# A decoder block in split float32: one contraction tile and four channel tiles multiplied whole

## The chip, the cores and the metric

The kernel runs on one core of a Trainium2 chip. The metric is the device time of one execution in microseconds; the kernel before has a median of 1739.6 us over 3 runs (1739.5 to 1740.47). The engines of the core are named PE (matrix multiply; PEld is its weight load), DVE (vector), ACT (activation and copy), POOL and SP (which here issues nearly all DMAs). Each works through its own instructions in order and waits for the others by semaphores.

## The reference, cut to what matters

One decoder layer on x of 256 tokens by 4096 channels, all in float32:

```
mod = silu(c) @ w_ada + b_ada             -> shift, scale, gate   (4096 -> 3 x 4096)
h   = rmsnorm(x) * (1 + scale) + shift
P   = h @ w_in                            (256 x 4096) @ (4096 x 14336)
y_A = a_b * conv3(a_c * a_x) * silu(a_z)              mixer A, 2048 channels
y_B = silu(layernorm(conv31(b_v * sigmoid(b_g)))) * silu(b_z)   mixer B, 2048 channels
out = rmsnorm(x + gate * ([y_A, y_B] @ w_out))        (256 x 4096) @ (4096 x 4096)
```

## The kernel before

**Split products.** The matrix products keep float32 accuracy by a split. Each weight tile (2 contraction tiles of 128 rows by 512 columns, a "step") is loaded as float32 into a buffer w_r of the pool "raws", which has four buffers. ACT casts it to float32r (w_h, L217) and DVE subtracts (w_l = w_r - w_h, L218). The activations h and y are split the same way (L250 on ACT, L253 on DVE). `products` then issues three matmuls for each contraction tile and each of the two token tiles: high by high, high by low, low by high (L244 to L246). w_h and w_l have three buffers each in the pool "split".

**Order of the work.** w_in is walked in seven blocks of contraction tiles (2, 4, 4, 4, 6, 6, 6 of the 32). In each block all 28 column tiles of 512 are visited; one visit is a "segment". A segment is seeded with the sum so far (L599) and taken off PSUM by ACT or DVE (L615, L610). The last block holds contraction tiles 26 to 31, so each of its 28 segments has three steps, and the third multiplies tiles 30 and 31. Its column tiles come in the order 20, 16, 21, 17, 22, 18, 23, 19, then four rounds of 4, 8, 12, 0 counted up, then 24 to 27. After it w_out is walked in two halves: first contraction tiles 0 to 15 (the channels of mixer A) for all eight output tiles ("pa", eight steps each, taken by L668), then tiles 16 to 31 (mixer B, "pb").

**What runs beside it.** During the last block and pa, the short convolution of mixer A (L438 to L444) makes y in tiles yfA, the convolution of 31 taps of mixer B runs tap by tap as a product on ACT (L500) and an addition on DVE (L503) or as one step on DVE (L496), and DVE sums the columns of the gate's weights (L271, 1 MB each). Two reductions on PE, mu_ps and var_ps (L525), belong to the layer norm, and gate_ps (L300) turns the finished gate.

**What sets the order.** The order on every engine is written by the program itself. `now` counts contraction tiles multiplied. `put` files work under a due count, and `run_due` issues it; the gate sums are fillers, issued when due or when the planner's account of DVE's time (`vec`, with LOW_PART for each subtracted contraction tile) and of the loads has room. `next_w` issues the load, cast and subtraction of a step two steps before its matmuls (AHEAD = 2). A tile of a pool takes the free buffer that was released longest ago, and its first writer waits for that buffer's last reader. The tiles h, x, y, the sums and the convolution's products share the pool "big" of 34 buffers.

Of the kernel before, what the change touches and what calls it, by code (L numbers as in the profile page):

```python
# [22 lines left out]
KT = D // P  # L23
# [49 lines left out]
def _segments():  # L73
# [35 lines left out]
def decoder_block(ctx: ExitStack, tc: tile.TileContext, x, c, w_mod, w_gate, w_in, w_out, xt, pk, final_g, out):  # L109
    nc = tc.nc  # L110
# [58 lines left out]
    plan = [(w_in[e], k, n) for _, e, k0, k1 in SEGS for k, n in _steps(k0, k1)]  # L169
    end_in = sum(n for _, _, n in plan)  # L170
    start_last = sum(k1 - k0 for b, _, k0, k1 in SEGS if b < len(BLOCKS) - 1)
    conv_end = end_in + CONV_END
    plan += [(w_out[dt], k0 + k, KD) for k0 in (0, KT // 2) for dt in range(NDT) for k in range(0, KT // 2, KD)]
    loaded = []
    step = 0
    now = 0
# [2 lines left out]
    vec = load = 0.0  # L179
# [9 lines left out]
    def run_due():  # L189
# [7 lines left out]
        while filler:  # L197
            due, mb, cost, f = filler[0]
            if due > now and (max(vec, t - SLACK) + cost > t + UNIT * KD or max(load, t - SLACK) + mb / RATE > t + UNIT):
                break  # L200
# [6 lines left out]
    def load_w(i):  # L207
        nonlocal vec, load
        src, k, n = plan[i]
        raw = raws.tile([P, KD, CT], F32, tag="r", name=f"w{i}_r")  # L210
        part = slice(k % KD, k % KD + n)
        nc.sync.dma_start(raw[:, part], src[k // KD][:, part])
        if 0 <= i - len(plan) + KT // 2 // KD < HOLD:
            hi, lo = (bigt(f"w{i}_{t}", (P, KD, CT), F32R) for t in "hl")
        else:
            hi, lo = (split.tile([P, KD, CT], F32R, tag=t, name=f"w{i}_{t}") for t in "hl")
        nc.scalar.copy(hi[:, part], raw[:, part])  # L217
        nc.vector.tensor_tensor(out=lo[:, part], in0=raw[:, part], in1=hi[:, part].bitcast(F32), op=ALU.subtract)  # L218
        t = FIRST + UNIT * now
        vec = max(vec, t - SLACK) + LOW_PART * n  # L220
        load = max(load, t - SLACK) + W_LOAD * n / RATE
        return hi, lo

    def next_w():

# [8 lines left out]

    def products(ps, act, parts, k0, n, first, last, tokens=range(NS), seeded=False):

        hi, lo = parts
        for k in range(k0, k0 + n):
            f, l = first and k == k0, last and k == k0 + n - 1
            for s in tokens:  # L240
                out = ps[s] if isinstance(ps, list) else ps[:, s]
                ah, al = (act[k][:, h, s * P:(s + 1) * P] for h in range(2))
                i = k % KD
                nc.tensor.matmul(out, ah, hi[:, i], start=f, stop=False, skip_group_check=seeded)  # L244
                nc.tensor.matmul(out, ah, lo[:, i], start=False, stop=False, skip_group_check=seeded)  # L245
                nc.tensor.matmul(out, al, hi[:, i], start=False, stop=l, skip_group_check=seeded)  # L246

    def hi_part(dst, src):

        nc.scalar.copy(dst[:, :, 0], src)  # L250

    def lo_part(dst, src):
        nc.vector.tensor_tensor(out=dst[:, :, 1], in0=src, in1=dst[:, :, 0].bitcast(F32), op=ALU.subtract)  # L253
# [55 lines left out]
    act_h = {}  # L309

    def h_steps(ks):

        st = {}
        n = len(ks)

        def fetch():
            st["x"] = bigt(f"xc{ks[0]}", (P, n, S))
            nc.sync.dma_start(st["x"], xt[:, ks[0]:ks[0] + n])

        def by_token():  # L320
            nc.vector.tensor_tensor(out=st["x"], in0=st["x"], in1=rstd.unsqueeze(1).broadcast_to([P, n, S]), op=ALU.mult)

        def by_channel():
            for i, k in enumerate(ks):
                nc.scalar.activation(out=st["x"][:, i], in_=st["x"][:, i], func=AF.Identity, scale=gscT[:, k:k + 1], bias=modT[:, k:k + 1])

        def high():
            st["h"] = bigt(f"hT{ks[0]}", (P, n, 2, S), F32R)
            hi_part(st["h"], st["x"])

        def low():
            lo_part(st["h"], st["x"])
            for i, k in enumerate(ks):
                act_h[k] = st["h"][:, i]

        return [(fetch, 0.0), (by_token, 0.3 * n + 0.05), (by_channel, 0.0), (high, 0.0), (low, 0.3 * n + 0.05)]

# [5 lines left out]
    for q in range(4):  # L343
        for s in range(NS):
            t = bigt(f"xn{q}_{s}", (P, 1024))
# [23 lines left out]
    v, y, t = (tiny[:, i] for i in range(3))  # L369
# [25 lines left out]
    vec = load = FIRST - SLACK  # L395
# [19 lines left out]
    yT = {}  # L415
# [7 lines left out]
    def silu_gate_A(i):  # L423

        p, q = acc[4 + i], acc[i]
        tiles, pss = {}, {}

        def turn(j):
            cc = slice(j * P, (j + 1) * P)
            ps = pss[j] = misc(f"psA{4 * i + j}", (P, 2, S))  # L430
            for s in range(NS):
                nc.tensor.transpose(ps[:, 0, s * P:(s + 1) * P], p[:, s, cc], ident)
                nc.tensor.transpose(ps[:, 1, s * P:(s + 1) * P], q[:, s, cc], ident)

        def tap(j):
            if j % 2 == 0:
                tiles[j // 2] = bigt(f"yfA{i}_{j}", (P, 2, S))
            nc.scalar.activation(out=tiles[j // 2][:, j % 2], in_=pss[j][:, 0], func=AF.Copy, scale=caw[:, 4 * i + j, 2:3])  # L438

        def rest(j):  # L440
            y, ct = tiles[j // 2][:, j % 2], 4 * i + j
            for sh in (1, 2):
                nc.vector.scalar_tensor_tensor(out=y[:, sh:], in0=pss[j][:, 0, :S - sh], scalar=caw[:, ct, 2 - sh:3 - sh], in1=y[:, sh:], op0=ALU.mult, op1=ALU.add)
            nc.vector.tensor_tensor(out=y, in0=y, in1=pss[j][:, 1], op=ALU.mult)  # L444
            if j % 2 == 1:
                hi, lo = split_y(2 * i + j // 2, tiles[j // 2])
                put(now + 2, hi)
                put(now + 4, lo, 0.65)

        t = now + 4  # L450
        for j in range(4):
            put(t + A_STEP * j, lambda j=j: turn(j))
            put(t + A_STEP * j + 0.1, lambda j=j: tap(j))
            put(t + A_STEP * j + 2, lambda j=j: rest(j), 1.15)
# [177 lines left out]
    for n, (b, e, k0, k1) in enumerate(SEGS):  # L632
        steps = _steps(k0, k1)
        for j, (k, m) in enumerate(steps):
            parts = begin_step()
# [11 lines left out]
    for i in range(4):  # L647
        for h in range(2):
            t = end_in + NORM_AT + NORM_STEP * (19.5 + 2 * i + h)
# [20 lines left out]
    for dt in range(NDT):  # L670
        ps = pst(f"pa{dt}")
        for k in range(0, KT // 2, KD):
            parts = begin_step()
# [91 lines left out]
    for s in range(NS):  # L765
# [4 lines left out]
        v, y, t = (const.tile([P, 1], F32, name=f"o_{n}{s}") for n in "vyt")  # L770
# [47 lines left out]
```

## Time and profile before

| | |
|---|---|
| median of 3 runs | 1739.6 us |
| the profiled execution | 1735.66 us, span 1733.9 us |
| PE busy | 1635.9 us (94%) |
| DVE busy | 1398.1 us (81%) |
| ACT busy | 1171.9 us (68%) |
| DMA | 526.02 MB, mean 303 GB/s |
| mean granted PE clock | 0.991 |

The page's slices of the span:

```profile
PE   6999999999999999999999999989988988899997
DVE  6888877778777877778777778899999999875666
ACT  5787667666677666666656666999977775564444
DMA  9998999999999999999999999665666778667775
```

Each column is a fortieth of the span (43.3 us), each digit the busy share in tenths. The shares of the whole span are means over parts with different limits, so a change in one part is read from that part alone. A matmul's duration includes a drain that overlaps the next one, so for its cost one looks at the time from start to next start.

### The profile page before, as it was taken

What the parts mean: (1) busy time and instruction counts of PE and PEld (TensorE: products, weight loads), DVE (VectorE), ACT (ScalarE), POOL (GpSimd) and SP (SyncE); (2) the same over time, 40 slices, a digit from 0 to 9 for tenths busy, and PEclk for the clock granted to TensorE, in tenths of its full rate; (3) what the DMA queues carried; (4) which work ended last, traced back from release to release, by engine and by line L of the source; (5) the groups of instructions that cost most, each with busy time, mean ns of one, the idle gap of its engine ahead of it and who ended that gap; (6) DMA issues with size and microseconds to landing.
All of it is one profiled execution on the core that took longest, in us unless ns stands there. A gap on an engine that the chain in (4) does not pass through costs nothing.

```text
span 1733.9 us, 20044 instructions
## 1 busy us (share of the span) xinstructions
PE 1635.9 (94%) x7069; PEld 1321.2 (76%) x7069; DVE 1398.1 (81%) x1409; ACT 1171.9 (68%) x1525; POOL 1.0 (0%) x8
## 2 busy tenths in 40 slices
PE   6999999999999999999999999989988988899997
PEld 3668878888788788887888887777766766778885
DVE  6888877778777877778777778899999999875666
ACT  5787667666677666666656666999977775564444
POOL 0000000000000000000000000000000000000000
PEclk9999999999999999999999999999999999999999
DMA  9998999999999999999999999665666778667775
GB/s 363 373 380 334 370 336 336 331 346 357 342 349 348 358 336 344 348 353 361 338 349 342 349 359 336 205 188 165 194 232 222 286 258 292 240 195 248 242 240 190
DMA packets 122284, 526.02 MB, mean 303 GB/s; under 512 B 13476, under 2 KB 13764, under 8 KB 97608
## 3 DMA queue, kind: packets, MB, share of 16 engines
q1 hardware_dynamic: 121992, 524.36, 83.7%
q8 instruction: 56, 0.92, 0.2%
q10 hardware_dynamic: 192, 0.39, 0.1%
q14 instruction: 44, 0.36, 0.1%
HBM read 520.48 MB, written 4.21 MB: 303 GB/s over the span
## 4 chain that ended last, share of the span: by engine, by line
PE 62%; DVE 19%; issue 8%; ACT 5%; DMA 5%; SPq 0%; DVEq 0%; ACTq 0%
PE ps L246 17%; PE ps L244 17%; PE ps L245 17%; DVE w_l L218 7%; DVE cv L503 4%; DMA w_r<-in_w_in 4%; PE pb L245 3%; PE pb L244 3%; PE pb L246 3%; ACT w_h L217 2%; DVE gate L271 2%; DVE cv L496 2%; DMA mod<-in_w_mod 1%; DVE mod L271 1%; ACT acc L615 1%
## 5 line engine op out<-in xcount | busy, mean ns | idle before, releaser
L218 DVE TENSOR_TENSOR w_l<-w_r,w_h 128x1024 fp32r<-128x1024 f32 (+1 forms) x591 | 704.9, 1196 | 302.6 <-ACT w_h L217 301.9
L217 ACT CAST w_h<-w_r 128x1024 fp32r<-128x1024 f32 (+1 forms) x591 | 609.4, 1032 | 499.8 <-PE ps L246 325.6
L245 PE MATMUL ps<-w_l,hT 128*128 128x512 f32 x1792 | 703.9, 393 | 24.0 <-DVE w_l L218 23.8
L244 PE MATMUL ps<-w_h,hT 128*128 128x512 f32 x1792 | 705.6, 394 | 15.2 <-ACT hT L250 7.9
L246 PE MATMUL ps<-w_h,hT 128*128 128x512 f32 x1792 | 702.5, 392 | 9.5 <-DVE hT L253 9.4
L245 PEld LDWEIGHTS ps<-w_l,hT 128*128 128x128 f32 x1792 | 338.6, 189 | 102.6 <-DVE w_l L218 33.4
L244 PEld LDWEIGHTS ps<-w_h,hT 128*128 128x128 f32 x1792 | 338.4, 189 | 92.5 <-ACT hT L250 8.6
L246 PEld LDWEIGHTS ps<-w_h,hT 128*128 128x128 f32 x1792 | 338.4, 189 | 83.8 <-DVE hT L253 13.5
L615 ACT ACTIVATE acc<-ps 128x1024 f32<-128x1024 f32 x178 | 181.4, 1019 | 0.0
L599 ACT COPY ps<-acc 128x1024 f32<-128x1024 f32 x162 | 164.1, 1013 | 0.0
L500 ACT ACTIVATE pr<-uT,pks 128x254 f32<-128x254 f32 (+23 forms) x384 | 159.3, 496 | 0.0
L271 DVE CUSTOM_DVE_ANT_0 mod<-mod,cB,pks 128x2048 f32<-128x2048 f32 x64 | 150.2, 2346 | 2.7 <-DMA mod<-in_w_mod 2.7
L271 DVE CUSTOM_DVE_ANT_0 mod<-mod,cB,pts 128x2048 f32<-128x2048 f32 x64 | 150.2, 2347 | 2.6 <-DMA mod<-in_w_mod 2.6
L245 PE MATMUL pa<-w_l,yT 128*128 128x512 f32 x256 | 103.1, 403 | 14.2 <-DVE w_l L218 14.2
L503 DVE TENSOR_TENSOR cv<-cv,pr 128x1020 f32<-128x1020 f32 (+11 forms) x96 | 111.3, 1159 | 0.9
L244 PE MATMUL pa<-w_h,yT 128*128 128x512 f32 x256 | 102.6, 401 | 0.0
L246 PE MATMUL pa<-w_h,yT 128*128 128x512 f32 x256 | 101.1, 395 | 0.0
L244 PE MATMUL pb<-w_h,yT 128*128 128x512 f32 x256 | 99.8, 390 | 0.0
L246 PE MATMUL pb<-w_h,yT 128*128 128x512 f32 x256 | 99.6, 389 | 0.0
L245 PE MATMUL pb<-w_l,yT 128*128 128x512 f32 x256 | 99.6, 389 | 0.0
L271 DVE CUSTOM_DVE_ANT_0 gate<-gate,cB,pts 128x2048 f32<-128x2048 f32 x32 | 75.1, 2347 | 0.0
L271 DVE CUSTOM_DVE_ANT_0 gate<-gate,cB,pks 128x2048 f32<-128x2048 f32 x32 | 75.1, 2346 | 0.0
(112 smaller groups left out, 689.4 us busy)
## 6 DMA issues: line engine op xcount, KB each, us to landing
w_r<-in_w_in SPq DMA_DIRECT2D x433, 512.0 KB, 5.3
mod<-in_w_mod SPq DMA_DIRECT2D x128, 1024.0 KB, 7.2
gate<-in_w_gate SPq DMA_DIRECT2D x64, 1024.0 KB, 6.5
w_r<-in_w_out SPq DMA_DIRECT2D x128, 512.0 KB, 4.4
w_r<-in_w_in SPq DMA_DIRECT2D x30, 256.0 KB, 5.7
xn<-in_x SPq DMA_DIRECT2D x8, 512.0 KB, 5.8
xr<-in_x SPq DMA_DIRECT2D x8, 512.0 KB, 6.9
out<-o SPq DMA_DIRECT2D x16, 256.0 KB, 2.4
```

What stands on the lines that cost most here:

```text
L217: nc.scalar.copy(hi[:, part], raw[:, part])
L218: nc.vector.tensor_tensor(out=lo[:, part], in0=raw[:, part], in1=hi[:, part].bitcast(F32), op=ALU.subtract)
L244: nc.tensor.matmul(out, ah, hi[:, i], start=f, stop=False, skip_group_check=seeded)
L245: nc.tensor.matmul(out, ah, lo[:, i], start=False, stop=False, skip_group_check=seeded)
L246: nc.tensor.matmul(out, al, hi[:, i], start=False, stop=l, skip_group_check=seeded)
L271: nc.vector.tensor_tensor_reduce(out=raw, in0=raw, in1=cB[:, q * ROW:(q + 1) * ROW], scale=1.0, scalar=pt if q else bias, op0=ALU.mult, op ...
L496: nc.vector.scalar_tensor_tensor(out=o[:, j, sh:], in0=u[:, j, :S - sh], scalar=cbw[:, 4 * i + j, TAPS - 1 - sh:TAPS - sh], in1=o[:, j, sh ...
L500: nc.scalar.activation(out=pr[:, j, sh:], in_=u[:, j, :S - sh], func=AF.Copy, scale=cbw[:, 4 * i + j, TAPS - 1 - sh:TAPS - sh])
L503: nc.vector.tensor_tensor(out=o[:, :, sh:], in0=o[:, :, sh:], in1=pr[:, :, sh:], op=ALU.add)
L599: nc.scalar.copy(ps, acc[e])
L615: nc.scalar.activation(out=acc[e], in_=ps, func=func)
```

## The change

The last contraction tile of w_in (31) and four of w_out (12 to 15, mixer A's last channels) are multiplied whole: one float32 matmul of the unsplit activations by the unsplit weights w_r takes the place of three split ones. Nothing of those weights is cast or subtracted, and h of tile 31 and y of tiles 12 to 15 are not split. In the third step of a segment of the last block half of the weight tile is split and half is not; in pa the last two of eight steps are whole. The float32 tiles of x (two contraction tiles) and of y (yfA) are kept until their last matmul, and w_r until its step is multiplied. The planner counts LOW_PART only for what is subtracted.

```diff
+WHOLE_IN = (KT - 1,)
+WHOLE_OUT = (12, 13, 14, 15)
...
     def load_w(i):
         src, k, n = plan[i]
+        whole = WHOLE_IN if i < steps_in else WHOLE_OUT
+        ns = sum(j not in whole for j in range(k, k + n))
         raw = raws.tile([P, KD, CT], F32, tag="r", name=f"w{i}_r")
...
-        nc.scalar.copy(hi[:, part], raw[:, part])
-        nc.vector.tensor_tensor(out=lo[:, part], in0=raw[:, part], in1=hi[:, part].bitcast(F32), op=ALU.subtract)
+        if ns:
+            part = slice(k % KD, k % KD + ns)
+            nc.scalar.copy(hi[:, part], raw[:, part])
+            nc.vector.tensor_tensor(out=lo[:, part], in0=raw[:, part], in1=hi[:, part].bitcast(F32), op=ALU.subtract)
         t = FIRST + UNIT * now
-        vec = max(vec, t - SLACK) + LOW_PART * n
+        vec = max(vec, t - SLACK) + LOW_PART * ns
...
-        return hi, lo
+        return hi, lo, raw
...
     def products(ps, act, parts, k0, n, first, last, tokens=range(NS), seeded=False):
...
+                i = k % KD
+                if act[k].dtype == F32:
+                    nc.tensor.matmul(out, act[k][:, s * P:(s + 1) * P], raw[:, i], start=f, stop=l, skip_group_check=seeded)
+                    continue
                 ah, al = (act[k][:, h, s * P:(s + 1) * P] for h in range(2))
...
         def low():
-            lo_part(st["h"], st["x"])
+            lo_part(st["h"][:, :ns], st["x"][:, :ns])
             for i, k in enumerate(ks):
-                act_h[k] = st["h"][:, i]
+                act_h[k] = st["h"][:, i] if i < ns else st["x"][:, i]
...
-            if j % 2 == 1:
+            if ct in WHOLE_OUT:
+                yT[ct] = y
+            elif j % 2 == 1:
```

DVE, around the two whole steps of the second pa tile (weight tiles w477 and w478, tap additions cv3 and a gate sum between them), before:

```order
L218 TENSOR_TENSOR w476_l_10567<-w476_r_10564,w476_h_10566 128x1024
L503 TENSOR_TENSOR cv3_8688<-cv3_8688,pr3_1_10547 128x4x255
L271 ISA gate24_0_10576,pts_103<-gate24_0_10576,cB_104,pks_60 128x2048
L271 ISA pts_103 128x1
L218 TENSOR_TENSOR w477_l_10594<-w477_r_10591,w477_h_10593 128x1024
L503 TENSOR_TENSOR cv3_8688<-cv3_8688,pr3_2_10570 128x4x254
L218 TENSOR_TENSOR w478_l_10618<-w478_r_10615,w478_h_10617 128x1024
L503 TENSOR_TENSOR cv3_8688<-cv3_8688,pr3_3_10597 128x4x253
L218 TENSOR_TENSOR w479_l_10642<-w479_r_10639,w479_h_10641 128x1024
```

The same place on DVE now:

```order
L228 TENSOR_TENSOR w476_l_10425<-w476_r_10422,w476_h_10424 128x1024
L519 TENSOR_TENSOR cv3_8655<-cv3_8655,pr3_1_10405 128x4x255
L284 ISA gate24_0_10434,pts_103<-gate24_0_10434,cB_104,pks_60 128x2048
L284 ISA pts_103 128x1
L519 TENSOR_TENSOR cv3_8655<-cv3_8655,pr3_2_10428 128x4x254
L519 TENSOR_TENSOR cv3_8655<-cv3_8655,pr3_3_10451 128x4x253
L228 TENSOR_TENSOR w479_l_10492<-w479_r_10489,w479_h_10491 128x1024
```

The two subtractions are gone; the additions and the gate sum between them stand as they stood.

SP, the loads that follow the two whole steps w469 and w470 of the first pa tile, with what each waits for (the DMAHW names are semaphores of earlier DMAs), before:

```order
L212 DMA w471_r_10437<-in_w_out 128x1024 [waits DMAHW6_49,DVE_49]
L270 DMA gate23_0_10449<-in_w_gate 128x2048 [waits DMAHW4_49]
L212 DMA w472_r_10464<-in_w_out 128x1024 [waits DMAHW7_49,DVE_49]
L212 DMA w473_r_10489<-in_w_out 128x1024 [waits DMAHW1_49,DVE_49]
L212 DMA w474_r_10515<-in_w_out 128x1024 [waits DMAHW2_49,DVE_49]
L270 DMA gate23_1_10526<-in_w_gate 128x2048 [waits DMAHW0_49]
L212 DMA w475_r_10541<-in_w_out 128x1024 [waits DMAHW3_49,DVE_49]
```

The same loads on SP now:

```order
L217 DMA w471_r_10311<-in_w_out 128x1024 [waits DMAHW6_49,DVE_49]
L283 DMA gate23_0_10323<-in_w_gate 128x2048 [waits DMAHW4_49]
L217 DMA w472_r_10330<-in_w_out 128x1024 [waits DMAHW7_49,DVE_49]
L217 DMA w473_r_10347<-in_w_out 128x1024 [waits DMAHW3_49,DVE_49]
L217 DMA w474_r_10373<-in_w_out 128x1024 [waits DMAHW1_49,PE_49]
L283 DMA gate23_1_10384<-in_w_gate 128x2048 [waits DMAHW0_49]
L217 DMA w475_r_10399<-in_w_out 128x1024 [waits DMAHW2_49,PE_49]
```

The order of the loads is the same; w474 and w475 take the buffers that the whole steps held and wait for PE where they waited for DVE.

## Rows read from the trace of the kernel before

**Rows 1.** Windows: length, then busy us of each engine (instructions), granted clock, DMA share, GB/s.

```profile
core 0: us, PE busy (x) PEld busy (x) DVE busy (x) ACT busy (x) POOL busy (x), PEclk, DMA share, GB/s
1052.00:1096.00 44.00, 42.21 (x193) 34.35 (x192) 34.49 (x33) 32.48 (x47) 0.00 (x0) 1.00 0.82 295
1096.00:1250.00 154.00, 140.58 (x627) 111.69 (x626) 145.79 (x176) 147.74 (x268) 0.00 (x0) 1.00 0.59 184
1250.00:1331.60 81.60, 67.12 (x276) 52.73 (x275) 80.85 (x100) 65.04 (x120) 0.00 (x0) 0.92 0.65 226
1331.60:1461.00 129.40, 116.60 (x485) 92.08 (x485) 129.02 (x141) 96.85 (x175) 0.00 (x0) 0.97 0.77 276
1461.00:1546.20 85.20, 73.61 (x323) 57.80 (x322) 68.14 (x68) 45.17 (x59) 0.00 (x0) 0.98 0.69 231
1546.20:1722.00 175.80, 175.20 (x776) 144.53 (x774) 111.63 (x109) 86.26 (x109) 0.00 (x0) 1.00 0.70 228
```

**Rows 2.** Timeline, ACT: takes of segments and pa tiles: start us, us, instruction.

```profile
1095.97 1.03 ACT L615 ACTIVATE acc<-ps 128x1024 f32<-128x1024 f32 x1
...
1250.12 1.01 ACT L615 ACTIVATE acc<-ps 128x1024 f32<-128x1024 f32 x1
...
1460.92 1.01 ACT L668 COPY o<-pa 128x1024 f32<-128x1024 f32 x1
```

**Rows 3.** Waits from 1096 to 1250: total us, times, longest us.

```profile
PE ps L245 <- DVE w_l L218: 7.2, 8, 1.9
```

**Rows 4.** Waits from 1331.6 to 1461.

```profile
PE pa L245 <- DVE w_l L218: 12.8, 11, 2.1
```

**Rows 5.** Waits from 1461 to 1546.2.

```profile
PE mu_ps L525 <- DVE mu_t L520: 4.3, 1, 4.3
...
PE gate_ps L300 <- DVE gateT L271: 3.0, 1, 3.0
...
PE var_ps L525 <- DVE var_t L520: 2.4, 1, 2.4
```

**Rows 6.** Timeline, PE: first and last of 45 split matmuls in a row.

```profile
1080.02 0.39 PE L244 MATMUL ps<-w_h,hT 128*128 128x512 f32 x1
...
1089.99 0.39 PE L246 MATMUL ps<-w_h,hT 128*128 128x512 f32 x1
```

**Rows 7.** Timeline, PE: float32 matmuls of other shapes (in brackets the wait before).

```profile
3.03 13.99 PE L363 MATMUL cps<-crow,ones 1*128 1x512 f32 x16 [3.03 <-DMA crow<-in_c]
...
1497.82 1.13 PE L525 MATMUL var_ps<-var_t,mean_w 128*128 128x256 f32 x4 [2.35 <-DVE var_t L520]
```

**Rows 8.** Timeline, PE: after a long wait.

```profile
1275.75 0.79 PE L245 MATMUL ps<-w_l,hT 128*128 128x512 f32 x1 [3.50 <-DVE w_l L218]
1276.34 0.63 PE L246 MATMUL ps<-w_h,hT 128*128 128x512 f32 x1
...
1278.05 0.63 PE L244 MATMUL ps<-w_h,hT 128*128 128x512 f32 x1
...
1278.78 0.39 PE L246 MATMUL ps<-w_h,hT 128*128 128x512 f32 x1
```

**Rows 9.** Groups by shape, DVE and ACT: count, busy us, mean ns, idle before.

```profile
L218 DVE TENSOR_TENSOR w_l<-w_r,w_h 128x1024 fp32r<-128x1024 f32 x561 | 685.1, 1224 | 297.3 <-ACT w_h L217 296.7
L218 DVE TENSOR_TENSOR w_l<-w_r,w_h 128x512 fp32r<-128x512 f32 x30 | 20.3, 689 | 5.3 <-ACT w_h L217 5.2
...
L217 ACT CAST w_h<-w_r 128x1024 fp32r<-128x1024 f32 x561 | 591.0, 1055 | 487.5 <-PE ps L246 321.1 <-PE pb L246 65.8 <-PE pa L246 53.5
L217 ACT CAST w_h<-w_r 128x512 fp32r<-128x512 f32 x30 | 18.4, 617 | 12.3 <-DMA w_r<-in_w_in 7.7 <-PE ps L246 4.5
```

**Rows 10.** Timeline, DVE: a subtraction and the instruction after it.

```profile
1376.83 1.22 DVE L218 TENSOR_TENSOR w_l<-w_r,w_h 128x1024 fp32r<-128x1024 f32 x1
1377.96 1.21 DVE L503 TENSOR_TENSOR cv<-cv,pr 128x1012 f32<-128x1012 f32 x1
```

**Rows 11.** DMA issues from 1050 to 1331: count, KB each, median us to landing.

```profile
w_r<-in_w_in SPq DMA_DIRECT2D x78, 512.0 KB, 3.9
gate<-in_w_gate SPq DMA_DIRECT2D x15, 1024.0 KB, 6.1
```

**Rows 12.** DMA issues from 1331 to 1546.

```profile
w_r<-in_w_out SPq DMA_DIRECT2D x65, 512.0 KB, 4.4
```

More of the change, by code (lines that the diff above doesn't have):

```diff
@@ L173, in decoder_block @@
     plan += [(w_out[dt], k0 + k, KD) for k0 in (0, KT // 2) for dt in range(NDT) for k in range(0, KT // 2, KD)]
+    steps_in = sum(len(_steps(k0, k1)) for _, _, k0, k1 in SEGS)
     loaded = []
@@ L212, in load_w @@
         nc.sync.dma_start(raw[:, part], src[k // KD][:, part])
-        if 0 <= i - len(plan) + KT // 2 // KD < HOLD:
+        hi = lo = None
+        if not ns:
+            pass
+        elif 0 <= i - len(plan) + KT // 2 // KD < HOLD:
             hi, lo = (bigt(f"w{i}_{t}", (P, KD, CT), F32R) for t in "hl")
@@ L235, in products @@
     def products(ps, act, parts, k0, n, first, last, tokens=range(NS), seeded=False):
-        hi, lo = parts
+        hi, lo, raw = parts
         for k in range(k0, k0 + n):
@@ L241, in products @@
                 out = ps[s] if isinstance(ps, list) else ps[:, s]
+                i = k % KD
+                if act[k].dtype == F32:
+                    nc.tensor.matmul(out, act[k][:, s * P:(s + 1) * P], raw[:, i], start=f, stop=l, skip_group_check=seeded)
+                    continue
                 ah, al = (act[k][:, h, s * P:(s + 1) * P] for h in range(2))
-                i = k % KD
                 nc.tensor.matmul(out, ah, hi[:, i], start=f, stop=False, skip_group_check=seeded)
@@ L314, in h_steps @@
         n = len(ks)
+        ns = sum(k not in WHOLE_IN for k in ks)
         def fetch():
@@ L328, in high @@
             st["h"] = bigt(f"hT{ks[0]}", (P, n, 2, S), F32R)
-            hi_part(st["h"], st["x"])
+            hi_part(st["h"][:, :ns], st["x"][:, :ns])
         def low():
-            lo_part(st["h"], st["x"])
+            lo_part(st["h"][:, :ns], st["x"][:, :ns])
             for i, k in enumerate(ks):
-                act_h[k] = st["h"][:, i]
+                act_h[k] = st["h"][:, i] if i < ns else st["x"][:, i]
         return [(fetch, 0.0), (by_token, 0.3 * n + 0.05), (by_channel, 0.0), (high, 0.0), (low, 0.3 * n + 0.05)]
```

## The prediction

> **What bounds the kernel now.** I began with the slices of the page: DMA is near full until slice 25 and falls after it, and DVE reads 9 from slice 27 to 34. So the program has three parts with different limits. The change touches only the last block of six (28 segments) and the first half of the output projection (eight tiles "pa"), so I cut exactly that stretch into windows [rows 1]. The cuts lie at the takes that end the fifth segment of the block (1095.97), the twenty-first (1250.12) and the fifth pa tile (1460.92), counted in the code's order [rows 2].
>
> - 1052 to 1096 us, 5 segments: PE busy 42.2 of 44.0, DVE 34.5. PE is the limit.
> - 1096 to 1250, 16 segments: PE 140.6, DVE 145.8, ACT 147.7 of 154.0. All three are nearly full.
> - 1250 to 1331.6, 7 segments: DVE 80.9 of 81.6, PE 67.1, and the clock is 0.92. DVE is the limit.
> - 1331.6 to 1461, 5 pa tiles: DVE 129.0 of 129.4, PE 116.6. DVE is the limit.
> - 1461 to 1546.2, 3 pa tiles: PE 73.6 of 85.2, DVE 68.1. Neither is full: PE waits here three times for a result of DVE that its next instruction in order needs.
> - 1546.2 to 1722, the second half of the projection: PE 175.2 of 175.8. PE is the limit, and the change leaves it alone.
>
> The waits agree. PE waits for the low parts w_l of DVE: 7.2 us in the second stretch, 12.8 in the fourth [rows 3, 4]. In the fifth it waits 4.3 for mu_t, 3.0 for gateT, 2.4 for var_t [rows 5].
>
> **What one matmul costs.** A split product is three matmuls. From 1080.02 to 1089.99 there are 45 starts in a row, 44 steps of 0.2266 us [rows 6], so one token of one contraction tile costs 0.680 us. A float32 matmul of 128x512 with full rows is not in this trace. Two relatives are. The eight matmuls "cps" (one row by 512 columns, float32) appear as 16 records in 13.99 us: two records each, 0.862 us per record once 0.2 for the last one's drain is taken off [rows 7] (0.63 of duration less 0.43 of step [rows 8]). The two "var_ps" matmuls (256 columns) are four records in 1.13 us, 0.242 per record after 0.16 of drain (0.39 less 0.23 [rows 6, 7]). Per 512 columns that is 0.484, so cps at 0.862 must have run at the lower clock, 1.2 GHz; at 2.4 GHz it is 0.431 per record, 0.862 per matmul. The split matmuls at half clock step by 0.4275 (1276.34 to 1278.05 in four steps [rows 8]); four such passes at full clock are 0.855. So the added PE time is 0.175 from that side, 0.18 from cps, 0.288 from var_ps (which started after a wait). I take 0.18, because cps has the longest run of records. There are 28 x 2 = 56 such matmuls in the block and 8 x 4 x 2 = 64 in pa: 120 x 0.18 = 21.6 us on PE, 0.36 per segment and 1.44 per pa tile.
>
> The Trainium skill, "FP8 and Floating Point Precision", section TensorE Precision Notes, says that a true float32 product takes 4 passes through the array. The trace agrees in kind (two records, each of double length), but at the pace of the split matmuls four passes would be 0.906, an estimate from that page, so 0.226 more each and 27 us in all; the sum below would then come out at -8.0 in place of -12.9 (106 of the 120 lie where PE can become the limit, 106 x 0.046 = 4.9).
>
> **What leaves DVE and ACT.** A subtraction of 128x1024 has 1224 ns, of 128x512 689 [rows 9], so each segment frees 0.535 us of DVE. The cast goes from 1055 to 617 ns, 0.438 us of ACT. In pa two of eight steps lose the whole subtraction, which is 1.13 us from start to next start (1376.83 to 1377.96 [rows 10]), so 2.26 per tile on DVE and 2.1 on ACT. Two splits of y go too, 0.69 each on DVE. The low part of h shrinks once; that is nothing here. The planner also issues two gate sums some 30 loads earlier in the block; DVE has them to do all the same, so I count the move at nothing. It gains a little if they land in the 8.2 us in which DVE is idle in the second stretch.
>
> **Stretch by stretch.**
> 1. 5 segments, PE the limit: 5 x 0.36 = **+1.8**.
> 2. 16 segments. PE becomes 140.6 + 5.8 = 146.4, ACT 147.7 - 7.0 = 140.7, DVE 145.8 - 8.6 = 137.2. PE alone allows 154.0 - 146.4 = -7.6; nothing at all is gained if the small waits of three full engines stay as they are. I take **-3**: today 154.0 is 6.3 above the fullest engine, and 151 keeps 4.6 of it.
> 3. 7 segments, DVE the limit with PE far behind (67.1 + 2.5): 7 x 0.535 = **-3.7**. Ends: -3.7 and -2.
> 4. 5 tiles. DVE sheds 5 x 2.26 + 1.4 = 12.7. PE is 116.6, less 3.9 that the half clock cost (0.03 x 129.4), plus 7.2: 119.9, so PE stops the gain at -9.5. I take **-7**, some 2.5 us of waits for w_l staying of 12.8. The lower end is -2.
> 5. 3 tiles: PE +4.3. The three waits hold 9.7 us and all are for DVE, which arrives 6.8 us lighter. Ends: +4.3 if they stay, -2.5 if 6.8 goes. I take **-1**.
> 6. The second half and the tail: 0. Their instructions are the same; I leave 1 us either way, since the last two whole steps of pa still hold buffers when it begins.
>
> Sum: 1.8 - 3 - 3.7 - 7 - 1 = -12.9; the ends add up to -21.5 and +2. The profiled execution took 1735.66 us (span 1733.9), which becomes 1722.8; the median of the runs, 1739.6, is 3.9 above it, so I forecast 1739.6 - 12.9 = **1726.7**.
>
> **The wait that the change adds.** A weight buffer ("raw", four of them) was free once DVE had subtracted; a whole or half whole one is free only when PE has multiplied it. In SP's queue the loads w474 and w475 now wait for PE. Behind them on SP stand the gate loads and all later weights. The other loads share the buffers that are left, three where they had four, so one can be issued only when the load three before it has been subtracted. In pa, where two whole steps are held, w473 even follows on w471, but DVE has no subtraction to do for 6.9 us of PE's time there, and w471's is done early. A load takes 3.9 us to land in the block and 4.4 in pa, a gate 6.1 [rows 11, 12]. Three steps of the second stretch are a segment, 154.0 / 16 = 9.6 us; less cast and subtraction (1.06 + 1.13) that leaves 7.4 us. So I cost the wait at nothing; rival C is what it costs if that cover goes.
>
> **Rivals.**
> A. *DVE's relief arrives whole.* The waits for mu_t, gateT and var_t shrink, the long gaps go, and the clock with them: after a gap of 3.50 us the next matmuls last 0.63 instead of 0.39 us [rows 8], and (1 - 0.92) x 81.6 + 3.9 = 10.4 us were lost so in stretches 3 and 4. For it: DVE never idles there. Against it: stretch 3 stays bound by DVE, so its clock is worth little. -21.5, and 2 more from the gate sums: 1716. The Trainium skill, "TensorE: Matmul & The Clock Gate", section HAM oscillation, has the same rule, that gaps between bursts bring the clock down and dense work keeps it up; rows 8 agree for one gap.
> B. *PE gives it all back.* At 0.288 per matmul PE takes 0.108 more each, 106 x 0.108 = 11.4 us outside stretch 3: -12.9 + 11.4 = -1.5, 1738. For it: var_ps at 1.13 us. Against it: cps.
> C. *Slower: the weights come late.* Place: each segment's load that waits on a subtraction only three steps before. If landing takes 8.4 us, each of 28 segments waits 1 us: +28, net +15, 1755. It decides from a landing of 7.4 us on, and turns the sign from about 7.9. For it: SP's queue is strictly in order and a gate load can stand ahead. Against it: the median of 3.9, with DMA at 0.59 to 0.77 of its time there.
> D. *Slower: the clock falls in the float32 stretches.* cps stayed at the lower clock for 14 us with PE busy. One pa tile has 6.9 us of float32 in a row; half of it at half clock is +3.5 us, 8 x 3.5 = 28, net +15 as well. Against it: cps has one row of 128.
> That the change does less than it says I hold for excluded: on DVE the subtractions of the whole steps are gone from the order, and SP's loads wait for PE in their place.
>
> **Chances.** Forecast (-6 to -20) 0.55; A 0.16; B 0.14; C 0.10; D 0.05. A difference under 0.2% (3.5 us) can't be told from none here. B falls half on "same", a third on "faster", the rest on "slower"; the forecast's thin edge adds 0.02 to "same". Faster 0.55 + 0.16 + 0.05 - 0.02 = 0.74; same 0.07 + 0.02 = 0.09; slower 0.02 + 0.10 + 0.05 = 0.17. The range takes in A and B and half of the way to C: 1713 to 1742. The likeliest case's own range is 1719 to 1734.
>
> **What would show it.** Right: the subtraction count at 128x1024 falls by 28 + 16 and that at 128x512 rises by 28; float32 records of about 0.6 us, two per matmul, 0.43 apart; pa tiles about 24.5 us apart where they are 25.9 (129.4 / 5); PE's waits for w_l in 1331 to 1461 down from 12.8 to 3 or so; the second half still 175 us. Wrong: float32 records more than 0.46 apart (B), ACT or DVE waiting for DMA w_r in the block (C), a granted clock below 0.9 in pa (D), or PE waits for w_l as long as before while DVE is no longer full, which would mean that something other than DVE's load set them.

## The result and the profile after

The changed kernel takes 1716.65 us (median of four runs, 1716.42 to 1720.08); the kernel before, on the same chip, 1739.55 (1737.53 to 1740.47). The ratio is 0.9875, 95% interval 0.9857 to 0.9892: 21.8 us less, 19 to 25. The forecast was 12.9 less. The sign and the range held, the size did not; it is the size of rival A.

The profiled execution after has 1716.42 us (span 1714.6), so the two traces differ by 19.2 us. The two traces already stand 3.1 us apart where the block begins (its first split matmul starts at 1048.83 before and at 1051.92 after), ahead of every changed matmul, so 1052.00 before is 1055.08 after. Windows of the trace after, cut at the same places of the program as [rows 1]: length, then busy us of each engine (instructions), granted clock, DMA share, GB/s.

```profile
1055.08:1098.80 43.72, 42.66 (x178) 31.61 (x177) 31.65 (x33) 30.31 (x46) 0.00 (x0) 1.00 0.77 289
1098.80:1253.05 154.25, 147.37 (x596) 107.22 (x595) 141.70 (x180) 141.26 (x268) 0.00 (x0) 0.99 0.55 191
1253.05:1324.30 71.25, 65.51 (x267) 48.21 (x265) 70.15 (x93) 61.29 (x118) 0.00 (x0) 0.98 0.68 240
1324.30:1448.60 124.30, 119.87 (x449) 83.67 (x448) 122.06 (x133) 85.55 (x165) 0.00 (x0) 1.00 0.77 286
1448.60:1526.90 78.30, 73.84 (x294) 52.05 (x293) 61.85 (x63) 40.44 (x55) 0.00 (x0) 1.00 0.71 253
1526.90:1702.80 175.90, 175.27 (x775) 144.46 (x773) 109.05 (x105) 84.95 (x107) 0.00 (x0) 1.00 0.71 230
```

Against [rows 1], stretch by stretch:

| stretch | before | after | change | forecast |
|---|---|---|---|---|
| 1: 5 segments | 44.00 | 43.72 | -0.3 | +1.8 |
| 2: 16 segments | 154.00 | 154.25 | +0.25 | -3 |
| 3: 7 segments | 81.60 | 71.25 | -10.35 | -3.7 |
| 4: 5 pa tiles | 129.40 | 124.30 | -5.1 | -7 |
| 5: 3 pa tiles | 85.20 | 78.30 | -6.9 | -1 |
| 6: second half | 175.80 | 175.90 | +0.1 | 0 |

The six add up to -22.3, and with the 3.1 us ahead of the block to the 19.2 between the traces. That head start is scatter: in the fourteen traces of this document the last take before the block starts between 1041.8 and 1045.1, whatever was changed.

Two terms were much too small, 3 and 5, and the +1.8 of stretch 1 is not seen in its length. In stretch 3 DVE is still the limit (70.15 of 71.25), but it has 10.7 us less to do, not 3.7. In stretch 5 PE was idle for 11.6 us before and is for 4.5 now.

The float32 matmuls, on PE's timeline after (start us, us, instruction; a row can hold several records) and by their records' durations (ns, min/median/max):

```profile
1392.84 7.03 PE L254 MATMUL pa<-w_r,yfA 128*128 128x512 f32 x16
1399.31 0.79 PE L257 MATMUL pa<-w_h,yT 128*128 128x512 f32 x1
1399.94 0.40 PE L258 MATMUL pa<-w_l,yT 128*128 128x512 f32 x1
```

```profile
L254 PE MATMUL pa<-w_r,yfA x128: 590/592/595, 1343.8 to 1526.2; 128*128 128x512 f32 x128
L254 PE MATMUL ps<-w_r,xc x112: 589/592/1058, 1060.5 to 1324.1; 128*128 128x512 f32 x112
```

128 records for the 64 matmuls of pa: two each. Sixteen last 7.03 us; less the last one's 0.592, fifteen steps are 0.429 each, 0.858 per matmul against 0.680 for the split product [rows 6]: 0.178 more, where 0.18 was taken.

The waits after, in stretches 2, 4 and 5 in turn (engine and line, waited for: us in total, times, longest), beside [rows 3 to 5]; the last fence is ACT's wait for weights in stretch 4 before:

```profile
ACT w_h L227 <- DMA w_r<-in_w_in: 4.0, 3, 2.2
...
PE ps L258 <- DVE w_l L228: 2.7, 5, 1.2
```

```profile
ACT w_h L227 <- DMA w_r<-in_w_out: 32.5, 15, 5.6
...
PE pa L258 <- DVE w_l L228: 4.4, 5, 2.1
```

```profile
PE mu_ps L541 <- DVE mu_t L536: 3.1, 1, 3.1
PE psZ L597 <- ACT gate_row L316: 1.0, 1, 1.0
PE var_ps L541 <- DVE var_t L536: 0.3, 1, 0.3
```

```profile
ACT w_h L217 <- DMA w_r<-in_w_out: 0.4, 1, 0.4
```

PE's wait for w_l went from 7.2 to 2.7 in stretch 2 and from 12.8 to 4.4 in stretch 4. In stretch 5 the waits for gateT (3.0) and nearly all of that for var_t (2.4) are gone. New are ACT's waits for weights to land: 32.5 us in stretch 4, where before it waited 0.4, and 4.0 in stretch 2. The prediction had named such waits in the block as a sign of rival C.

DVE's subtractions after, by shape (count, busy us, mean ns, idle before), answer to [rows 9]:

```profile
L228 DVE TENSOR_TENSOR w_l<-w_r,w_h 128x1024 fp32r<-128x1024 f32 x517 | 631.5, 1223 | 304.2 <-ACT w_h L227 303.8
...
L228 DVE TENSOR_TENSOR w_l<-w_r,w_h 128x512 fp32r<-128x512 f32 x58 | 39.6, 687 | 7.8 <-ACT w_h L227 7.5
```

561 - 44 = 517 and 30 + 28 = 58, as forecast.

### The profile page after: what moved, and what is told of

Read it like the earlier page. It is cut to its first block, busy times and chain, and to the rows that moved or that the text cites. A ratio compares the mean times of both kernels' runs of the same rounds, so it can differ in the third digit from the quotient of the medians.

```text
span 1714.6 us, 19750 instructions
## 1 busy us (share of the span) xinstructions
PE 1647.5 (96%) x6949; PEld 1297.7 (76%) x6949; DVE 1365.2 (80%) x1391; ACT 1140.6 (67%) x1507; POOL 1.0 (0%) x8
## 4 chain that ended last, share of the span: by engine, by line
PE 69%; DVE 12%; DMA 8%; ACT 5%; issue 5%; SPq 0%; DVEq 0%; ACTq 0%
PE ps L259 17%; PE ps L258 17%; PE ps L257 17%; DMA w_r<-in_w_in 5%; DVE w_l L228 5%; PE pb L258 3%; PE pb L257 3%; PE pb L259 3%; PE pa L254 2%; ACT w_h L227 2%; DVE cv L519 2%; DMA mod<-in_w_mod 2%; DVE cv L512 1%; PE pa L258 1%; PE pa L259 1%
## 5 line engine op out<-in xcount | busy, mean ns | idle before, releaser
L228 DVE TENSOR_TENSOR w_l<-w_r,w_h 128x1024 fp32r<-128x1024 f32 (+1 forms) x575 | 670.3, 1169 | 312.0 <-ACT w_h L227 311.4
L227 ACT CAST w_h<-w_r 128x1024 fp32r<-128x1024 f32 (+1 forms) x575 | 578.4, 1007 | 511.2 <-PE ps L259 324.1
L257 PE MATMUL ps<-w_h,hT 128*128 128x512 f32 x1736 | 691.3, 398 | 16.2 <-ACT hT L263 8.6
L258 PE MATMUL ps<-w_l,hT 128*128 128x512 f32 x1736 | 681.5, 393 | 11.3 <-DVE w_l L228 11.0
L259 PE MATMUL ps<-w_h,hT 128*128 128x512 f32 x1736 | 681.0, 392 | 7.1 <-DVE hT L266 6.9
L257 PEld LDWEIGHTS ps<-w_h,hT 128*128 128x128 f32 x1736 | 327.9, 189 | 95.0 <-ACT hT L263 9.3
L258 PEld LDWEIGHTS ps<-w_l,hT 128*128 128x128 f32 x1736 | 327.9, 189 | 89.9 <-DVE w_l L228 19.6
L259 PEld LDWEIGHTS ps<-w_h,hT 128*128 128x128 f32 x1736 | 327.8, 189 | 78.2 <-DVE hT L266 10.2
L258 PE MATMUL pa<-w_l,yT 128*128 128x512 f32 x192 | 75.7, 394 | 4.4 <-DVE w_l L228 4.4
L257 PE MATMUL pa<-w_h,yT 128*128 128x512 f32 x192 | 78.5, 409 | 0.0
L259 PE MATMUL pa<-w_h,yT 128*128 128x512 f32 x192 | 74.9, 390 | 0.0
```

## The experiments

Each was timed in five rounds beside the kernel before, on the same chip. "Less" and "more" are against that kernel, from the ratio. A profiled execution can stand several us off its kernel's median (before: 1735.66 against 1739.55), so totals are taken from the ratios and the traces say where. For that, all kernels were cut at the same takes (the last take before the block, those of [rows 2], and the last take of the block and of pa). The labels are explained run by run below; the "hold" is the time that a raw buffer stays taken until PE has multiplied it. The lengths are:

| kernel | ratio, interval | 1 | 2 | 3 | 4 | 5 |
|---|---|---|---|---|---|---|
| before | 1 | 54.1 | 154.1 | 83.0 | 127.9 | 86.4 |
| after | 0.9875 (0.9857 to 0.9892) | 53.8 | 154.3 | 72.0 | 123.5 | 78.2 |
| old gate places | 0.9888 (0.9874 to 0.9902) | 53.9 | 152.7 | 76.1 | 124.0 | 80.6 |
| gates moved only | 0.9986 (0.9975 to 0.9998) | 54.2 | 156.8 | 77.2 | 127.6 | 91.3 |
| block only | 0.9965 (0.9952 to 0.9978) | 53.9 | 154.1 | 74.0 | 129.1 | 90.6 |
| pa only | 0.9910 (0.9896 to 0.9925) | 54.1 | 155.6 | 81.0 | 121.8 | 80.0 |
| price only | 1.0036 (1.0023 to 1.0048) | 55.3 | 158.5 | 81.8 | 131.2 | 84.9 |
| relief only | 0.9798 (0.9783 to 0.9813) | 53.3 | 148.3 | 72.4 | 120.4 | 78.3 |
| no hold | 0.9841 (0.9825 to 0.9857) | 53.9 | 152.5 | 73.5 | 119.2 | 79.1 |
| last 12 segments | 0.9894 (0.9878 to 0.9910) | 54.1 | 158.7 | 72.1 | 123.4 | 78.3 |
| pa: first five | 0.9900 (0.9885 to 0.9916) | 53.9 | 153.6 | 74.1 | 122.2 | 87.3 |
| pa: last three | 0.9922 (0.9909 to 0.9935) | 53.8 | 154.1 | 73.3 | 129.8 | 83.6 |
| spaced | 0.9835 (0.9820 to 0.9850) | 53.9 | 154.0 | 73.6 | 118.3 | 77.0 |
| spaced, from segment 5 | 0.9839 (0.9824 to 0.9854) | 53.7 | 154.3 | 73.6 | 118.3 | 78.6 |

Each length is of one trace and good to about 2 us. After and spaced have the same program up to the second pa tile, yet their stretch 3 is 72.0 and 73.6: the take falls at another place of DVE's work (in stretch 3 DVE starts 17 tap additions after, 18 in spaced, 19 before). Some expectations reckon with +2.0 in stretch 1; they go by a window of the trace after that begins 2.3 us too early, and the figure is -0.3.

My theory was that the two missing sizes came from the two gate sums, which the changed account issues earlier, and from DVE's relief ahead of the three waits of stretch 5. The rivals: the stretches gain by the relief alone, wherever the gate sums stand; or PE's price shows only in part.

**The gate sums.** Two runs: the change with the planner's old account, and the kernel before with the new one.

```diff
-        vec = max(vec, t - SLACK) + LOW_PART * ns
+        vec = max(vec, t - SLACK) + LOW_PART * n
```

> The change, but the planner counts every weight tile as subtracted, so each gate sum stands where it stood before. Theory G (the two gate sums that went from the third stretch, where DVE is full, to the second, where it has room, are worth their 2 x 2.35 us): 1716.7 + 4.7 = 1721.4. Theory S (only the subtractions count; the place of the sums is worth nothing, as the prediction had it): 1716.7 within 1.5. By G, DVE in the third stretch is again some 4.7 us longer.

> The kernel before, all products split, but the planner's account is that of the change, so the two gate sums are issued at the change's places. Theory G: 1739.5 - 4.7 = 1734.8, all of it in the third stretch. Theory S: 1739.5 within 1.5.

Measured: 19.5 less and 2.4 less. Both lie about halfway between the two figures. DVE's rows in stretch 3 (between the takes) show what moved; first the old gate places, then after:

```profile
L284 DVE CUSTOM_DVE_ANT_0 gate<-gate,cB,pts 128x2048 f32<-128x2048 f32 x4 | 9.4, 2345 | 0.0
L284 DVE CUSTOM_DVE_ANT_0 gate<-gate,cB,pks 128x2048 f32<-128x2048 f32 x3 | 7.0, 2345 | 0.0
```

```profile
L284 DVE CUSTOM_DVE_ANT_0 gate<-gate,cB,pts 128x2048 f32<-128x2048 f32 x3 | 7.0, 2346 | 0.0
...
L284 DVE CUSTOM_DVE_ANT_0 gate<-gate,cB,pks 128x2048 f32<-128x2048 f32 x2 | 4.7, 2348 | 0.0
```

Seven sums against five, 4.7 us of DVE. Stretch 3 is 4.1 us shorter for it (76.1 to 72.0), and stretch 2, which takes them, 1.6 longer (152.7 to 154.3). All else that DVE does between these takes is the same in both. So the move buys 4.1 where DVE is the limit and pays 1.6 where it has some room. In these two stretches that is a net 2.5, and 2.4 by the second run's ratio, whose interval (0.3 to 4.4 less) leaves out both nothing and the full 4.7. The intervals of the change with and without the move overlap, and stretch 5 answers both ways (80.6 to 78.2 in the first pair, 86.4 to 91.3 in the second), so the size for the whole kernel stays rough.

**One half alone.**

```diff
-WHOLE_OUT = (12, 13, 14, 15)
+WHOLE_OUT = ()
```

> Only contraction tile 31 of the block is whole; pa is split as before. By the stretches of the two traces (+2.0, +0.3, -10.4): 1739.5 - 8.1 = 1731.4. By the prediction's terms (+1.8 - 3 - 3.7): 1734.6. If pa gains from DVE coming less late out of the block, it is below 1731.

```diff
-WHOLE_IN = (KT - 1,)
+WHOLE_IN = ()
```

> Only channel tiles 12 to 15 in pa are whole; the block is as before. By the stretches of the two traces (-5.1 - 6.9): 1739.5 - 12.0 = 1727.5. By the prediction's terms (-7 - 1): 1731.5. If part of pa's gain came out of the block, it is between the two.

Measured: 6.1 less and 15.7 less; together 21.8, the whole. Pa gained twice its terms (-8). The block's total is near its terms (+1.8 - 3 - 3.7 = -4.9), but by luck: its stretches show -0.2, 0.0 and -9.0, and 1.2 and 4.2 of that are lost again in stretches 4 and 5 (129.1 against 127.9, 90.6 against 86.4). The windows of stretch 5, block alone, then pa alone:

```profile
1456.19:1545.80 89.61, 78.25 (x324) 61.09 (x323) 68.45 (x68) 45.30 (x59) 0.00 (x0) 0.92 0.67 220
```

```profile
1457.27:1537.40 80.13, 75.70 (x296) 53.47 (x295) 62.24 (x63) 40.55 (x55) 0.00 (x0) 0.98 0.68 248
```

Block alone has the three waits of before (4.2, 3.0, 2.3 us) and a granted clock of 0.92; pa alone has 3.1, none and 0.3, and 0.98. With the block alone PE idles as long as before (89.61 - 78.25 = 11.4 us; [rows 1]: 11.6), but the same work keeps it busy 4.6 us longer (324 records in 78.25 us; before, 323 in 73.61).

**Which pa tiles.** The four channel tiles whole only in the first five pa tiles, then only in the last three, y kept in both forms:

```diff
+WHOLE_DT = (0, 1, 2, 3, 4)        # the mirror: (5, 6, 7)
...
-                if act[k].dtype == F32:
-                    nc.tensor.matmul(out, act[k][:, s * P:(s + 1) * P], raw[:, i], start=f, stop=l, skip_group_check=seeded)
+                if k in now_whole:
+                    nc.tensor.matmul(out, unsplit[id(act), k][:, s * P:(s + 1) * P], raw[:, i], start=f, stop=l, skip_group_check=seeded)
...
```

> The change, with channel tiles 12 to 15 whole only in the first five pa tiles and split as before in the last three (their y is kept in both forms, so all splits of y are made); block and gate places as in the change (after: 1716.7). By the prediction's terms 1 of the 8 of the pa tiles comes back: about 1718. If the last stretch gains 7 by its own relief (waits for var_t and gateT go because DVE has less to do there): about 1723 and those two waits are back. If it gains because DVE comes with less behind it out of the first five: the waits stay away, 1717 to 1719.

> The mirror: channel tiles 12 to 15 whole only in the last three pa tiles, split as before in the first five; the rest as in the change. By the prediction's terms 7 of the 8 come back: about 1724. If the last stretch gains by its own relief: 1721 to 1722, without the waits for var_t and gateT. If it gains because of what DVE saved earlier: 1728, with the waits.

Measured: 1721.98 and 1726.27. The waits of PE in stretch 5, first five whole:

```profile
PE mu_ps L548 <- DVE mu_t L543: 3.1, 1, 3.1
PE gate_ps L320 <- DVE gateT L291: 3.0, 1, 3.0
PE var_ps L548 <- DVE var_t L543: 2.4, 1, 2.4
PE pa L265 <- DVE w_l L235: 1.4, 2, 0.8
```

and last three whole:

```profile
PE mu_ps L548 <- DVE mu_t L543: 4.3, 1, 4.3
PE psZ L604 <- ACT gate_row L323: 1.0, 1, 1.0
PE pa L265 <- DVE w_l L235: 0.4, 1, 0.4
PE var_ps L548 <- DVE var_t L543: 0.3, 1, 0.3
```

With the first five whole, DVE comes early into stretch 5 and still gains nothing there (87.3): the waits for gateT and var_t are back to the tenth, and the clock is 0.94. With the last three whole both waits are gone, although nothing was saved in stretch 4. So these two waits depend on what DVE has to do in stretch 5, not on how early it comes in; the wait for mu_t does shrink by coming early (4.3 to 3.1). The whole change is 5.3 us faster than the first run and 9.6 faster than the second (4.4 and 8.2 by the ratios): the last three tiles are worth some 5, where the forecast had 1, and the first five 8 to 10, where it had 7. Coming early is worth more in stretch 5 than mu_t's 1.2, 83.6 against 78.2; the granted clock there is 0.96 against 1.00, and no run parts the two.

**Price and relief apart.** Price: the float32 matmuls, but every cast and subtraction still made.

```diff
-        ns = sum(j not in whole for j in range(k, k + n))
+        ns = n
...
-        vec = max(vec, t - SLACK) + LOW_PART * ns
+        vec = max(vec, t - SLACK) + LOW_PART * n
...
```

Relief: nothing cast or subtracted, but three float32r matmuls per product.

```diff
-                    nc.tensor.matmul(out, act[k][:, s * P:(s + 1) * P], raw[:, i], start=f, stop=l, skip_group_check=seeded)
+                    other = act[k - 1 if act is act_h else 0]
+                    for q in range(3):
+                        nc.tensor.matmul(out, other[:, 1, s * P:(s + 1) * P], other, start=f and q == 0, stop=l and q == 2, skip_group_check=seeded)
```

> The change's 120 float32 matmuls, but every cast and subtraction of the kernel before is still made (their results for these tiles are not read) and the planner's account is as before. PE's price alone. If the price binds only where PE is the limit (theory R): +1.8 in 1052-1096, about half of 16 x 0.36 = 2.9 in 1096-1250, 0 to 1 in 1250-1331.6, 0 in 1331.6-1461 where DVE sets the pace, some 2 in 1461-1546: about +8, near 1748. If each of the 120 x 0.18 us shows (theory P): +21.6, near 1762. If PE's price is hidden everywhere: 1740 to 1742.

> The change's relief alone: no cast, subtraction or split for these tiles, but PE keeps three float32r matmuls for each product (their operands are low halves of other tiles, so the output is not the reference's, and the weights of these steps are loaded but not read, which also takes away the hold of the raw buffer). Theory R: the stretches with DVE as limit stay as in the change (about 71 and 124 us), the PE-limited ones give the price back: 2 in 1052-1096, some 4 in 1096-1250, 1 and 0.5 in the next two, 3 in the last: about 10 below the change, near 1706. Theory P (price shows everywhere): 21.6 below, near 1695. Price hidden everywhere: 1716.7.

Measured: 6.3 more (5.7 by the medians) and 35.1 less. Theory R, not P: of the 21.6 us that PE has more to do, 6 show when DVE's load stays, and 7.5 when it is gone (relief only against no hold, below, which differ in nothing else of weight: 0.9798 and 0.9841). Most of what shows is in stretch 2, 148.3 against 152.5 with no hold: 4.2 of the 5.8 that PE has more there. The windows of stretch 2, relief only, then no hold:

```profile
1096.80:1245.10 148.30, 138.99 (x625) 111.55 (x624) 140.74 (x179) 141.66 (x268) 0.00 (x0) 1.00 0.62 198
```

```profile
1096.71:1249.19 152.48, 145.76 (x596) 106.33 (x595) 141.69 (x180) 141.50 (x268) 0.00 (x0) 1.00 0.61 194
```

The rest lies beside DVE's work. Two things blur the price-only run. Its matmuls read the raw weights too, so its 6 us contain the hold. And its stretch 4 is 3.3 us longer (131.2), where theory R had 0; stretches 4 and 5 together are 1.8 longer, of the 11.5 us that PE has more to do there.

**The hold.** The float32 matmuls read activations in place of the raw weights, so that no load waits for PE:

```diff
-                    nc.tensor.matmul(out, act[k][:, s * P:(s + 1) * P], raw[:, i], start=f, stop=l, skip_group_check=seeded)
+                    nc.tensor.matmul(out, act[k][:, s * P:(s + 1) * P], pairs[id(act), k], start=f, stop=l, skip_group_check=seeded)
...
```

> The change, but its float32 matmuls read h's and y's own pairs as the moving operand in place of the raw weights (so the output is not the reference's): PE's work, the casts, subtractions and gate places are as in the change, only the raw buffer is no longer held until PE has multiplied it. If the hold is free, as the prediction has it: 1716 to 1717. If the loads that wait for PE (ACT waits 32.5 and 17.4 us for them in the pa tiles) cost time: 4 to 10 us less, 1707 to 1713.

Measured: 1713.5, some 3 us below the change by the medians and 5.9 by the ratios, whose intervals just touch. Stretch 4 is 119.2 against 123.5. What SP waits for there (us, times, longest), after:

```profile
SPq L217 <- DVE w_l L228: 72.7, 30, 5.7
SPq L217 <- PE pa L254: 20.5, 8, 7.1
```

With no hold the second row is gone, and ACT waits 8.0 us for w_r instead of 32.5:

```profile
ACT w_h L227 <- DMA w_r<-in_w_out: 8.0, 5, 2.7
```

So the hold is not free in pa: two whole steps stand one behind the other, two of the four raw buffers are held at once, and SP waits up to 7.1 us for PE with a load. Nor is it free in the block: in stretch 2 after, SP waits 32.5 us for PE, and the stretch is 154.3 (153.6 to 154.3 in the five kernels with the same program there) against 152.5. One reserve: a whole step's weights are read by nobody in this run, so its buffer is free as soon as the load has landed, earlier than that of a split step.

The lengths of the table, taken apart by cause (differences of one trace each, so good to about 2 us; the sums are the safer):

| stretch | relief (relief only less before) | PE's price (no hold less relief only) | hold (after less no hold) |
|---|---|---|---|
| 1 | -0.8 | +0.6 | -0.1 |
| 2 | -5.8 | +4.2 | +1.8 |
| 3 | -10.6 | +1.1 | -1.5 |
| 4 | -7.5 | -1.2 | +4.3 |
| 5 | -8.1 | +0.8 | -0.9 |
| sum | -32.8 | +5.5 | +3.6 |
| by the ratios | -35.1 | +7.5 | +5.9 |

**Two versions.** Tile 31 whole only in the last 12 segments, to take back PE's price in stretches 1 and 2:

```diff
+WHOLE_FROM = 16
...
+        now_whole = whole if of_step[i] else ()
+        ns = sum(j not in now_whole for j in range(k, k + n))
```

> The change, with tile 31 left whole only in the last 12 of the 28 segments (in the first 16 it is split as before), gate sums at the change's places, pa tiles as in the change. If relief is worth something only where DVE is the limit: the +2.05 of 1052-1096 goes, PE is 11 x 0.36 = 4 us less busy in 1096-1250 and DVE 11 x 0.535 = 5.9 busier, the last 7 segments keep their gain: 1712 to 1715. If the last segments gain because DVE came with less behind it out of 1096-1250: 1718 to 1722.

Measured: 1722.79, 6 us slower than the change by the medians and 3 by the ratios, whose intervals overlap. That is just above the rival's 1722, but not for its reason: stretch 3 keeps its 72.1, and stretch 2 is 158.7, 4.4 longer than after. PE is busy 3 us less there (144.4 against 147.4) and the stretch grows, with DVE busy 5.8 us more (147.6 against 141.7): PE waits 9.8 us for w_l where after it waits 2.7:

```profile
PE ps L265 <- DVE w_l L235: 9.8, 10, 2.7
```

So the relief is needed in stretch 2 as well. That it makes the room for the two gate sums fits the run with the gates moved only, whose stretch 2 is 2.7 longer than before (156.8 against 154.1); the 12 segments with the old gate places were not run.

Then the whole steps set apart, which came from the run with no hold:

```diff
+SPACED = (0, 2, 4, 12, 6, 8, 10, 14)
...
+def _order(k0, dt):
+    return SPACED if k0 == 0 and dt else range(0, KT // 2, KD)
...
-        for k in range(0, KT // 2, KD):
+        for j, k in enumerate(_order(0, dt)):
...
```

> The change, with the two whole weight pairs of each pa tile (from the second on) no longer one behind the other at its end but at the fourth and the eighth step: not two raw buffers in a row are held until PE has multiplied them, and DVE's work is spread. If the hold is what the run without a hold gained (some 4 us in the first five pa tiles): 1712 to 1714. If that run's gain was something else: 1716 to 1718.

> The spaced order and, beside it, tile 31 split as before in the first 5 of its 28 segments, where PE sets the pace and the change cost 2 us: 1.8 less than the spaced order alone, 1710 to 1712, if both terms hold. If DVE comes out of these segments with more behind it (5 x 0.535 = 2.7): no gain, 1712 to 1716.

Measured: 1711.71 and 1711.24. The spaced order beats both kernels: 28.7 less than before, and its interval (0.9820 to 0.9850) lies wholly below that of the change (0.9857 to 0.9892). Its windows of stretches 4 and 5, and SP's wait for PE in stretch 4:

```profile
1324.00:1442.33 118.33, 116.76 (x440) 82.15 (x439) 117.43 (x129) 84.63 (x165) 0.00 (x0) 1.00 0.83 302
1442.33:1519.37 77.04, 74.63 (x299) 53.41 (x298) 62.77 (x64) 40.48 (x54) 0.00 (x0) 1.00 0.73 257
```

```profile
SPq L223 <- PE pa L260: 14.5, 8, 3.2
```

Still eight waits, but none over 3.2 us where there were 7.1; PE's wait for w_l falls to 1.4 us, and stretch 4 is 118.3, about as with no hold (119.2). The hold may not be the whole reason: in stretches 3 to 5 spaced is 4.8 us shorter than after, no hold 1.9. The order also spreads DVE's relief over the tile, and no run parts the two. Splitting the first five segments again adds nothing: stretch 1 is 53.7 against 53.9, so the change had cost it no 2 us to win back.

## Why the prediction came out as it did

The direction stood because the limits were read right: DVE in stretches 3 and 4, its late results in 5, PE in 1 and 6. By its terms:

- **The price of a float32 matmul**, 0.18 us, measured 0.178. It came from the matmuls cps, read as run at the lower clock [rows 7, 8]. The trace's granted clock does not show that (it reads 1.00 from 3.03 to 17.02), but it reads 1.00 from 30.9 to 36.1 as well, where split matmuls step by 0.427; so the step decides, and 2 x 0.429 bears it out. Rival B, by var_ps, falls. The Trainium skill's four passes ("FP8 and Floating Point Precision", section TensorE Precision Notes) fit the trace if a record is two of them, at 0.2145 us each; what was too high was to take them at the split matmuls' pace, 0.906.
- **Stretch 1**, +1.8: -0.3. PE does pay: from the block's first matmul to the transposes (psU) behind the fifth segment it takes 45.9 us where it took 44.6, and 46.5 with the price only. But the take of that segment starts 0.9 us after, where before ACT was 2.5 behind:

```profile
1093.43 0.60 PE L468 MATMUL psU<-ident,acc 128*128 128x128 f32 x4
1095.97 1.03 ACT L615 ACTIVATE acc<-ps 128x1024 f32<-128x1024 f32 x1
```

```profile
1097.84 0.60 PE L484 MATMUL psU<-ident,acc 128*128 128x128 f32 x4
1098.76 1.02 ACT L631 ACTIVATE acc<-ps 128x1024 f32<-128x1024 f32 x1
```

- **Stretch 6**, 0: +0.1.
- **Stretch 2**, -3: +0.25. The failed sentence is "so I count the move at nothing". The two sums (4.7 us) land here; with the old gate places the stretch is 152.7, 1.4 shorter than before. The other 1.6 are the price, which shows to 4.2 of 5.8, and the hold, 1.8 here, which the term had at nothing.
- **Stretch 3**, -3.7: -10.35. The same sentence, and the larger half of the miss. The two sums leave a stretch whose limit is DVE, and 4.1 us go with them. With old gate places it still lost 6.9, more than 3.7. Of the other 3.2, 0.6 is one of the two splits of y, which the prediction had put into stretch 4. The rest, 2.6, is no gain: one subtraction, one tap addition (1.1 us each) and the first 0.4 us of another, which DVE did before the last take of the block, now come behind it, and stretch 4 does them. DVE around that take (ACT), before and after:

```profile
1330.46 1.15 DVE L503 TENSOR_TENSOR cv<-cv,pr 128x956 f32<-128x956 f32 x1
1331.53 1.22 DVE L218 TENSOR_TENSOR w_l<-w_r,w_h 128x1024 fp32r<-128x1024 f32 x1
1332.66 1.15 DVE L503 TENSOR_TENSOR cv<-cv,pr 128x952 f32<-128x952 f32 x1
1333.07 1.02 ACT L615 ACTIVATE acc<-ps 128x1024 f32<-128x1024 f32 x1
```

```profile
1325.07 1.01 ACT L631 ACTIVATE acc<-ps 128x1024 f32<-128x1024 f32 x1
1325.12 1.15 DVE L519 TENSOR_TENSOR cv<-cv,pr 128x956 f32<-128x956 f32 x1
1326.18 1.22 DVE L228 TENSOR_TENSOR w_l<-w_r,w_h 128x1024 fp32r<-128x1024 f32 x1
```

With the 4.1 of the sums this makes the 11.0 that the stretch lost by the takes.
- **Stretch 4**, -7: -5.1. The DVE side was right: w_l waits at 4.4 where about 2.5 were left, pa tiles 24.7 us apart (123.5 / 5) where 24.5 were forecast. It is short by the 2.6 us taken over from stretch 3, and by the hold, which "I cost the wait at nothing" left out: without it the stretch is 4.3 shorter, 1.9 over stretches 3 to 5. The argument held 7.4 us, what three steps of the segments leave, against landings of 3.9 to 4.4; but in pa the hold keeps two buffers at once.
- **Stretch 5**, -1: -6.9, outside even its own ends (+4.3 and -2.5). The failed step is the size: I set PE's price of 4.3 against the waits, taking the price as paid in full. It was nearly hidden: with the relief it shows to 0.8 (78.3 against 79.1). And the waits for gateT and var_t went because DVE has less to do in this stretch, shown by the two runs on the pa tiles; 5.4 us of waits became 0.3, while the one for psZ grew from 0.3 to 1.0.

Rival A had the size, with half its reason: waits and gate sums as it says, and the clock is 1.00 or 0.98 where it was 0.97 and 0.92. How much of the gain is the clock itself no run separates. Rival C (weights late) is true in kind and small, 3 to 6 us, in pa and in the segments; it did not turn the sign: ACT waits 32.5 us for weights in stretch 4, PE 4.4 for what comes of them. Rival D is refuted: a pa tile has 7 us of float32 in a row at a granted clock of 1.00.

Summed by cause: relief 35.1 less (the moved gate sums in it), PE's price 7.5 back, the hold some 6 back (3 by the medians): 21.7 less. The forecast counted the price in full where PE was close to the limit, and no waits behind DVE beyond its busy time.

## What to carry to other kernels

Where work is moved off the engine that sets the pace, cost whatever a planner moves with it: here fillers of 4.7 us were worth 4.1 in the stretch that they left, bound by that engine, and cost 1.6 where they landed. An added duration on an engine that waits for another shows only in part (here 6 to 8 of 21.6 us). A buffer held longer costs (here 3 to 6 us), and two holds in a row are worth setting apart. And two traces are to be cut at the same instruction: the window that began 2.3 us too early made stretch 1 look just like its forecast.

## What was not expected of the hardware

A float32 128x512 matmul is two records 0.429 us apart, so a quarter of it takes 0.2145 us, less than the 0.2266 of a split matmul in the same place. There is no loss at the change-over: the second split matmul behind the sixteen records starts 1399.94 - 1392.84 = 7.10 us after their first, and 16 x 0.429 + 0.2266 is 7.09.

The same three waits of stretch 5 (4.2 to 4.3, 3.0, 2.3 to 2.4 us) stand beside a granted clock of 0.98 before, 0.92 with the block alone and 0.94 with the gates alone, and the stretch is 86.4, 90.6 and 91.3. What sets the clock apart there is open. With the block alone it goes with what was lost again in stretch 5: PE idles as long as before, and is busy 4.6 us longer with the same matmuls.
